# Seven half-sized products in place of eight for the gate and up products of four feed-forwards, with SBUF pools reopened by phase

## The chip, the cores and the metric

The kernel runs on one core of one Trainium2 chip. The metric is the device time of one execution in microseconds, median of three runs; lower is better. Before the change it is 1921.75 us (1920.16 to 1924.55).

## The reference, cut to what matters

A decoder trunk of two layers works on 512 tokens with 1024 features. Each layer has a feed-forward, a mixer and a second feed-forward, each added to the residual stream x (the feed-forwards with a factor of one half). The mixer of layer 0 is a gated linear recurrence, that of layer 1 a stick-breaking attention over keys and values that are projected once, from x after layer 0.

```python
D_MODEL, SEQ, D_FF = 1024, 512, 2816

def swiglu(h, w13, w2):
    gate, up = jnp.split(h @ w13, 2, axis=-1)
    return (jax.nn.silu(gate) * up) @ w2

for l in range(2):
    if l == 1:
        k_shared, v_shared = shared_kv(x, kv_norm, w_kv, k_norm)
    x = x + 0.5 * swiglu(rms_norm(x, ffn1_norm[l]), ffn1_w13[l], ffn1_w2[l])
    h = rms_norm(x, mix_norm[l])
    x = x + (rglru_block(h, ...) if l == 0 else stick_breaking_block(h, k_shared, v_shared, ...))
    x = x + 0.5 * swiglu(rms_norm(x, ffn2_norm[l]), ffn2_w13[l], ffn2_w2[l])
```

All data are float32.

## The kernel before, in words

Features lie on partitions and tokens along the free axis: x is eight tiles of 128 x 512. Each operand of a product is kept as two parts, a rounded one (hi, type fp32r) and the rest (lo). A product of weights and activations is three matmuls for each 128-wide step of the contraction: hi·hi, hi·lo, lo·hi (`steps`, lines 157 to 165). So a 128 x 512 output tile over 1024 features is 8 x 3 = 24 matmuls with 512 moving columns each, all recorded at line 111 (`mm`).

A feed-forward (`ffn`, lines 231 to 267) has 22 tiles of hidden features, cut into thirds of 8, 8 and 6. For each hidden tile it computes one gate tile and one up tile (two PSUM banks, 48 matmuls), then `swish`: VectorE multiplies both by the norm's factors r, ScalarE applies silu, VectorE multiplies the two, ScalarE rounds the product to hi and VectorE subtracts for lo. After a third's hidden tiles come eight down products, and VectorE adds each to x. With the last third, `after` squares the new x tile and splits x times gain into the next step's h. The factors r of the norm come after the first products (`Norm.rstd`), so the products run on x times gain without r.

Weights come in chunks of 128 x 1024 (`Weights`, lines 41 to 89): SyncE issues a DMA of 512 KB into a raw tile, ScalarE (or GpSimd) copies it to hi (line 55), VectorE subtracts for lo (line 59). Three buffers of each kind serve the whole program, and a chunk is emitted two chunks ahead of its use (`get`).

SBUF tiles come from pools that stay open for the whole program. In a pool, tiles of one tag share a number of buffers; a tile waits until a buffer of its tag is free, and buffers go out in the order in which they come free. The tiles h lie under tags `ah` and `al` (8 buffers each), the hidden tiles under `ch` and `cl` (8 each), temporaries `t0` and `t1` have two buffers each. PSUM has 8 banks under one tag.

The order of the instructions on each engine is made by the framework's list scheduler, which follows program order as priority among the instructions that its own estimate finds ready; two places fix it by hand (`manual_schedule`): the start and the first queries. On the chip each engine then keeps that order.

Between ffn2 of layer 0 and ffn1 of layer 1 stand the products of keys (8 x 24 matmuls) and values (192 matmuls). `v_out(1)` (lines 544 to 552), which evicts the second half of the values from PSUM, splits it and sends it to DRAM from two buffers of `t3` and two of `t4`, is called inside ffn1 of layer 1 after its first gate and up products, which need only h.

Of the kernel before, what the change touches and what calls it, by code (L numbers as in the profile page):

```python
# [12 lines left out]
P = 128  # L13
# [5 lines left out]
THIRDS = ((0, 8), (8, 16), (16, 22))  # L19
NH = 16  # L20
# [4 lines left out]
# queries of EARLY pairs come before the attention, the others among its units: from which step on, in how many steps  # L25
# [4 lines left out]
# columns of the packed vectors  # L30
# [4 lines left out]
# products of the recurrent block: inputs of the recurrence, its gates by block, the gate branch  # L35
# [5 lines left out]
class Weights:  # L41
    """Weight chunks in the order of their use: loaded ahead and split exactly into two 12-bit parts."""

    def __init__(self, nc, pool, plan, ahead):
        self.nc, self.pool, self.plan, self.ahead = nc, pool, plan, ahead
        self.ready, self.at = [], 0

    def tiles(self, j):
        return [self.pool.tile([P, 1024], dt, tag=t, name=f"{t}{j}") for t, dt in (("w_raw", F32), ("w_hi", F32R), ("w_lo", F32R))]
# [11 lines left out]
    def _emit(self, j):  # L61
        key, src, cols, hi_eng, lo_eng = self.plan[j]
        tiles = self.tiles(j)
        self.nc.sync.dma_start(tiles[0][:, :cols], src)
# [17 lines left out]
    def get(self, key):  # L82
        while len(self.ready) < min(len(self.plan), self.at + 1 + self.ahead):
# [5 lines left out]
        return hi, lo  # L89


@with_exitstack
def trunk(ctx, tc, a, out):
# [4 lines left out]
    hp = ctx.enter_context(tc.tile_pool(name="hp", bufs=8))  # L98
    wp = ctx.enter_context(tc.tile_pool(name="wp", bufs=3))
    tp = ctx.enter_context(tc.tile_pool(name="tp", bufs=2))  # L100
# [5 lines left out]

    def temp(tag, name, dt=F32, bufs=2, shape=None):
        return tp.tile(shape or [P, S], dt, tag=tag, name=name, bufs=bufs)
# [10 lines left out]
    plan = []  # L119
# [4 lines left out]
    def plan_ffn(n, l):  # L124
        for lo, hi in THIRDS:
            for i in range(lo, hi):
                plan_w((n, l, "g", i), a[f"{n}_w13"][l, i])
                plan_w((n, l, "u", i), a[f"{n}_w13"][l, FT + i])
# [3 lines left out]
    plan_ffn("ffn1", 0)  # L132
    for kind, m in RG_ORDER:
        plan_w((kind, m), a["w_ri"][m] if kind == "ri" else a["w_in"][m + (KT if kind == "rec" else 0)], hi="pool" if kind == "rec" else "act")
    for m in range(KT):
        plan_w(("wout", m), a["w_out"][m])
    plan_ffn("ffn2", 0)
# [5 lines left out]
    plan_ffn("ffn1", 1)  # L143
    for p in range(NPAIR):
        plan_w(("q", p), a["w_q"][p], hi="act" if p == 5 else "pool", lo="pool" if p == 5 else "dve")
    for m in range(KT):
        plan_w(("wo", m), a["w_o"][m], hi="pool" if m < 2 else "act")
    plan_ffn("ffn2", 1)
    W = Weights(nc, wp, plan, 2)

# [6 lines left out]
    def steps(ps, wt, ht, n=KT):  # L157
        """The products of ps = w.T h over n tiles of the contraction, w and h in two parts."""
# [12 lines left out]
    def product2(pa, wa, pb, wb, ht, full):  # L171
        """Two products of the same h; its last tile (or, in full, every tile) comes at the same time in both."""
# [6 lines left out]
    class Norm:  # L179
        """Sum of squares over the features of x and x * gain in two parts, tile by tile."""  # L180
# [15 lines left out]
        def rstd(self):  # L196
# [4 lines left out]
            # one table set for both functions, loaded between the last use of another and here  # L201
# [12 lines left out]
    def split_gain(xt, g, tag, name):  # L214
        hi = hp.tile([P, S], F32R, tag=tag + "h", name=name + "h")
        lo = hp.tile([P, S], F32R, tag=tag + "l", name=name + "l")
# [4 lines left out]
    def split(xt, tag, name, pool=False):  # L221
        hi = hp.tile([P, S], F32R, tag=tag + "h", name=name + "h")
        lo = hp.tile([P, S], F32R, tag=tag + "l", name=name + "l")
# [7 lines left out]
    def ffn(n, l, ht, rs, after, full=False):  # L231
        """x += 0.5 swiglu; rs() gives the norm's factors; after(m, x tile) once a tile of x is final."""
        r, queue = None, []

        def swish(i, pg, pu, act):
            tg, tu = temp("t0", f"tg{n}{l}{i}"), temp("t1", f"tu{n}{l}{i}")
# [4 lines left out]
            act.append(split(tu, "c", f"a{n}{l}{i}"))  # L241

        for lo_t, hi_t in THIRDS:
            act = []
            for i in range(lo_t, hi_t):
                pg, pu = psum(f"pg{n}{l}{i}"), psum(f"pu{n}{l}{i}")
# [30 lines left out]
    # the tensor engine's clock rises while the first data come in  # L277
# [15 lines left out]

    with tc.manual_schedule(engines={mybir.EngineType.DVE, mybir.EngineType.SP, mybir.EngineType.Activation}):
# [8 lines left out]
    def constants():  # L303
# [20 lines left out]
        # 0 where the key comes strictly before the query, else -1e30  # L324
# [28 lines left out]
        # gains of the per-head norms with the factors of the last Newton step (and 1/sqrt(head) for q)  # L353
# [6 lines left out]
    ffn("ffn1", 0, h, start, lambda m, t: n1.add(m, t, [(G_MIX[0], "a", h1)]), full=True)  # L360
# [6 lines left out]
    def conv(m, ps):  # L367
# [3 lines left out]
        xc[m] = hp.tile([P, S], F32, tag="bh", name=f"xc{m}")  # L371
# [20 lines left out]
    # p = tanh(-log_a / 2), q = 1 / (1 + p): a = 2 q - 1, sqrt(1 - a^2) = 2 sqrt(p) q  # L392
# [24 lines left out]
    def lru_3(b):  # L417
        for m in (2 * b, 2 * b + 1):
# [3 lines left out]
            hs[m] = hp.tile([P, S], F32, tag="bl", name=f"hs{m}")  # L422
# [43 lines left out]
    ffn("ffn2", 0, h2, n2.rstd, lambda m, t: n3.add(m, t, [(G_KV, "b", hkv), (G_FFN1[1], "a", h3)]))  # L466

# [6 lines left out]
    def head_norm(ps, r, g, name, dst, tags, qt=None):  # L474
        """psum * r, normed over each head's 64 rows, in two parts, to DRAM or to queries' tile qt; a generator of three stages."""
# [22 lines left out]
        if qt is not None:  # L498
            # both heads' rows in both halves of the partitions
# [20 lines left out]
    for p in range(NPAIR):  # L520
# [3 lines left out]
        if r3 is None:  # L524
            r3 = n3.rstd()
            # the same factors with tokens on partitions
# [12 lines left out]
        gen = head_norm(ps, r3, kg, f"k{p}", kd[p], ((tp, "t3"), (tp, "t4"), (tp, "rec"), (tp, "rec")))  # L539
# [34 lines left out]
    n4, h4 = Norm("n4"), []  # L574
    def finish_v():
        v_out(1, pvs[1])
        return r3
# [8 lines left out]
    ffn("ffn1", 1, h3, finish_v, after_ffn1)  # L586
# [8 lines left out]
    def load_pair(p):  # L595
        """Queries in both halves of the partitions; keys' two parts one above the other; values by chunk of keys."""
# [6 lines left out]
        for e in range(2):  # L603
            t = hp.tile([P, S], F32R, tag="cl", name=f"kp{p}{e}")
# [3 lines left out]
        for e in range(2):  # L608
            t = hp.tile([P, NCH, P], F32R, tag="cl", name=f"vp{p}{e}")
# [261 lines left out]
```

## Time and profile before

| | us |
|---|---|
| runs: median (lowest to highest) | 1921.75 (1920.16 to 1924.55) |
| profiled execution, span from first to last instruction | 1921.6 |
| TensorE matmuls busy | 1891.2 (98%), 8376 instructions |
| TensorE weight loads (beside the matmuls) | 1550.0 (81%), 8376 |
| VectorE busy | 1042.8 (54%), 1351 |
| ScalarE busy | 734.7 (38%), 1018 |
| GpSimd busy | 157.8 (8%), 196 |
| mean granted TensorE clock | 0.997 |

For the profiled execution no time is given apart from its span. Busy time of TensorE is taken from modelled ends, so two matmuls overlap in the records: the distance between the starts of neighbours is the time that one really takes. The same holds for VectorE, where the next instruction starts somewhat before the one before has ended in the records.

### The profile page before, as it was taken

To read this page: it belongs to the slowest core of one execution; us is meant where nothing else is said; L and a number is where in the kernel's file an instruction comes from. 1 tells how busy PE (TensorE), PEld (TensorE's weight loads), DVE (VectorE), ACT (ScalarE), POOL (GpSimd) and SP (SyncE) were. 2 spreads that over 40 slices of the span, in tenths; PEclk is the share of its full clock that TensorE was granted. 3 is DMA by queue.
4 is the path that set the end of the run, shared out by engine and by line. 5 is a ranking of instruction groups with operands and counts; after the bars stand their busy time and mean duration, and the time that the engine had idled before them with its cause. 6 is when DMAs were issued, how large, how long until landed. Compare 5 with 4: busy or idle time off the path is not lost.

```text
span 1921.6 us, 21311 instructions
## 1 busy us (share of the span) xinstructions
PE 1891.2 (98%) x8376; PEld 1550.0 (81%) x8376; DVE 1042.8 (54%) x1351; ACT 734.7 (38%) x1018; POOL 157.8 (8%) x196
## 2 busy tenths in 40 slices
PE   9999999999999999999999999999898999999999
PEld 7888888878788888888888888888676788888887
DVE  7434434797744354348744444346799854444343
ACT  6223223467543132236532223223588643222131
POOL 1000000031000000000200000000466400000000
PEclk9999999999999999999999999999999999999999
DMA  5322332322322233323562323324466222333322
GB/s 173 103 97 92 97 99 86 102 88 77 110 99 90 97 99 99 99 83 104 175 186 99 99 90 97 99 94 140 151 178 162 99 96 94 95 99 99 99 91 85
DMA packets 73092, 207.49 MB, mean 108 GB/s; under 512 B 7584, under 2 KB 17056, under 8 KB 72480
## 3 DMA queue, kind: packets, MB, share of 16 engines
q1 hardware_dynamic: 72704, 205.81, 33.8%
q8 instruction: 65, 1.06, 0.2%
q10 hardware_dynamic: 288, 0.32, 0.0%
q14 instruction: 35, 0.29, 0.0%
HBM read 189.85 MB, written 16.25 MB: 107 GB/s over the span
## 4 chain that ended last, share of the span: by engine, by line
PE 87%; DVE 7%; issue 2%; ACT 2%; POOL 2%; DMA 0%; POOLq 0%; DVEq 0%; ACTq 0%
PE pdffn L111 25%; PE pgffn L111 25%; PE puffn L111 25%; PE k L111 2%; PE v L111 2%; PE wout L111 2%; PE wo L111 2%; PE rec L111 2%; DVE spl L664 1%; DVE w_lo L59 1%; DVE t L664 1%; DVE sp L654 1%; PE z L111 1%; PE q L111 0%; POOL sph L661 0%
## 5 line engine op out<-in xcount | busy, mean ns | idle before, releaser
L55 ACT CAST w_hi<-w_raw 128x1024 fp32r<-128x1024 f32 (+1 forms) x313 | 321.4, 1030 | 979.4 <-PE pgffn L111 305.7
L59 DVE TENSOR_TENSOR w_lo<-w_raw,w_hi 128x1024 fp32r<-128x1024 f32 (+3 forms) x339 | 400.3, 1182 | 77.9 <-ACT w_hi L55 68.2
L239 DVE TENSOR_TENSOR tuffn<-puffn,rs_n 128x512 f32<-128x512 f32 x88 | 60.8, 691 | 242.3 <-PE puffn L111 242.3
L237 DVE TENSOR_TENSOR tgffn<-pgffn,rs_n 128x512 f32<-128x512 f32 x88 | 60.8, 691 | 216.1 <-PE pgffn L111 216.0
L265 DVE SCALAR_TENSOR_TENSOR x<-pdffn,x 128x512 f32<-128x512 f32 x72 | 49.8, 692 | 173.0 <-PE pdffn L111 172.8
L57 POOL TENSOR_SCALAR w_hi<-w_raw 128x1024 fp32r<-128x1024 f32 (+2 forms) x27 | 24.3, 903 | 751.5 <-PE pdffn L111 728.4
L240 DVE TENSOR_TENSOR tuffn<-tuffn,tgffn 128x512 f32<-128x512 f32 x88 | 60.7, 690 | 6.9
L238 ACT ACTIVATE tgffn<-tgffn 128x512 f32<-128x512 f32 x88 | 55.2, 627 | 5.4 <-DVE tgffn L237 5.1
L265 DVE SCALAR_TENSOR_TENSOR xr<-pdffn,xr 128x512 f32<-128x512 f32 x24 | 16.6, 692 | 70.9 <-PE pdffn L111 70.9
L481 POOL TENSOR_SCALAR thk<-tk 128x512 fp32r<-128x512 f32 x8 | 11.1, 1391 | 428.7 <-ACT tk L478 428.7
L111 PE MATMUL O<-t,vp 128*128 128x512 f32 (+1 forms) x144 | 41.2, 369 | 3.3 <-POOL t L661 1.9
L661 POOL TENSOR_SCALAR sph<-sp 128x512 fp32r<-128x512 f32 (+1 forms) x48 | 38.3, 802 | 23.4 <-DVE sp L657 12.8
L664 DVE TENSOR_TENSOR spl<-sp,sph 128x512 fp32r<-128x512 f32 (+1 forms) x48 | 38.8, 815 | 0.7 <-POOL sph L661 0.5
L661 POOL TENSOR_SCALAR t<-w 128x512 fp32r<-128x512 f32 (+1 forms) x48 | 37.5, 782 | 18.9 <-ACT w L685 15.7
L664 DVE TENSOR_TENSOR t<-w,t 128x512 fp32r<-128x512 f32 (+1 forms) x48 | 34.4, 717 | 3.3 <-POOL t L661 3.3
L111 PE MATMUL z<-qp,kp 128*128 128x256 f32 x192 | 33.5, 286 | 2.6 <-DVE qp L506 2.6
L111 PEld LDWEIGHTS z<-qp,kp 128*128 128x128 f32 x192 | 29.9, 191 | 6.3 <-DVE qp L506 3.4
L111 PEld LDWEIGHTS O<-t,vp 128*128 128x128 f32 x144 | 24.7, 188 | 11.1 <-DVE t L664 4.9
L187 ACT ACTIVATE sq_n<-x 128x512 f32<-128x512 f32 x40 | 25.1, 632 | 21.7 <-DVE x L265 18.0
L685 ACT ACTIVATE w<-z 128x512 f32<-128x512 f32 (+1 forms) x48 | 25.2, 525 | 16.2 <-PE z L111 15.5
L192 DVE TENSOR_TENSOR acc_n<-acc_n,sq_n 128x512 f32<-128x512 f32 x42 | 28.7, 684 | 0.1
L654 DVE SCALAR_TENSOR_TENSOR sp<-z,E 128x512 f32<-128x512 f32 (+1 forms) x48 | 28.3, 589 | 0.1
(1776 smaller groups left out, 5343.4 us busy)
## 6 DMA issues: line engine op xcount, KB each, us to landing
w_raw<-in_ffn_w SPq DMA_DIRECT2D x238, 512.0 KB, 3.3
w_raw<-in_ffn_w SPq DMA_DIRECT2D x32, 384.0 KB, 3.1
w_raw<-in_w_in SPq DMA_DIRECT2D x16, 512.0 KB, 3.2
qp<-qd SPq DMA_DIRECT2D x14, 512.0 KB, 5.4
w_raw<-in_w_out SPq DMA_DIRECT2D x8, 512.0 KB, 3.3
w_raw<-in_w_k SPq DMA_DIRECT2D x8, 512.0 KB, 3.2
w_raw<-in_w_v SPq DMA_DIRECT2D x8, 512.0 KB, 3.3
kp<-kd SPq DMA_DIRECT2D x32, 128.0 KB, 5.1
```

The costliest lines, as they stand in the source:

```text
L55: nc.scalar.copy(out=hi[:, cs], in_=raw[:, cs])
L59: eng.tensor_tensor(out=lo[:, cs], in0=raw[:, cs], in1=hi[:, cs].bitcast(F32), op=ALU.subtract)
L111: nc.tensor.matmul(o, l, r, start=start, stop=stop, skip_group_check=True)
L192: nc.vector.tensor_tensor(out=self.acc, in0=self.acc, in1=sq, op=ALU.add)
L237: nc.vector.tensor_tensor(out=tg, in0=pg, in1=r, op=ALU.mult)
L238: last_silu.append(nc.scalar.activation(out=tg, in_=tg, func=AF.Silu))
L239: nc.vector.tensor_tensor(out=tu, in0=pu, in1=r, op=ALU.mult)
L240: nc.vector.tensor_tensor(out=tu, in0=tu, in1=tg, op=ALU.mult)
L265: nc.vector.scalar_tensor_tensor(out=x[m], in0=pd, scalar=0.5, in1=x[m], op0=ALU.mult, op1=ALU.add)
L654: nc.vector.scalar_tensor_tensor(out=self.sp, in0=self.z, scalar=0.0, in1=ee, op0=ALU.max, op1=ALU.add)
L661: nc.gpsimd.tensor_scalar(out=hi, in0=src, scalar1=1.0, scalar2=0.0, op0=ALU.mult, op1=ALU.add)
L664: nc.vector.tensor_tensor(out=lo, in0=src, in1=hi.bitcast(F32), op=ALU.subtract)
```

## The change

The change works on pairs of hidden tiles. In 38 of the 44 pairs (11 in each of the four feed-forwards) the gate and up products of two tiles are computed by Strassen's scheme in the Winograd form: the weight matrix of the pair is cut into four blocks (two tiles of outputs by even and odd steps of the contraction), the activations into four blocks (even and odd steps by two halves of the tokens, 256 columns each), and seven products of blocks replace eight. The other six pairs (`PLAIN` = 4 tiles in three feed-forwards) stay as they were.

- The four blocks of a pair come by four DMAs of 512 KB, as before four chunks did. VectorE forms four sums of weight blocks (128 x 1024 each), and seven blocks in place of four are split into hi and lo. The pool has 7 raw, 5 hi and 5 lo buffers and works four chunks ahead in the feed-forwards, 3, 3, 3 and two in the mixers.
- A form (one of the seven products) is 2 (gate, up) x 4 steps x 3 = 24 matmuls of 256 columns. Seven forms use three PSUM banks; after each of the first six ScalarE or VectorE reads the bank into a tile `e`.
- Activations have to be normed and combined first: `normed` is called four times in a feed-forward (two tiles of x each) and makes seven blocks of 256 columns in two parts, with a tile `e` of 8 KB as scratch. It is called after the plain tiles (one call after each); in ffn1 of layer 1, which has no plain tiles, all four calls stand after `v_out(1)`, ahead of the first form. h for that feed-forward is no longer made.
- `swish`, `pair` and `normed` all take their scratch from one tag `e` with two buffers. Hidden tiles take the tags `ah` and `al`, the same eight buffers each as h.
- Pools for the activations' blocks, the weights and the scratch are opened and closed by phase; they lie on memory of the phase before, and a new tile waits for the tiles that lay there.

```diff
+PLAIN = {("ffn1", 0): 4, ("ffn2", 0): 4, ("ffn1", 1): 0, ("ffn2", 1): 4}
+BLOCKS = ("a11", "a21", "a22", "a12")
+SUMS = {"s3": ("a11", "a21"), "s1": ("a21", "a22"), "s2": ("s1", "a11"), "s4": ("s2", "a12"), **{b: None for b in BLOCKS}}
+FORMS = (("a11", "X", 4), ("s3", "Y", 0), ("s2", "X", 1), ("a12", "Z", 5), ("s1", "X", 2), ("a22", "Y", 3), ("s4", "X", 6))
+HS = S // 2
...
+    def block(self, j, name, src):
+        g = self.group
+        if name == FORMS[0][0]:
+            g.clear()
+            for k, b in enumerate(BLOCKS):
+                g[b] = self.tile("w_raw", f"w_{b}_{j}")
+                self.nc.sync.dma_start(g[b], src[k])
+        if name not in g:
+            p, q = SUMS[name]
+            p, q = (self.block(j, t, src) for t in (p, q))
+            g[name] = self.tile("w_raw", f"w_{name}_{j}")
+            self.nc.vector.tensor_tensor(out=g[name], in0=p, in1=q, op=ALU.add)
+        return g[name]
...
+    def phase_ffn():
+        close_pools()
+        cur.ht = open_pool("ht", hh=4, hl=4)
+        W.scope(open_pool("wf", w_raw=7, w_hi=5, w_lo=5), 4, plan_marks.pop(0))
+        cur.ep = None
+    def phase_mix():
+        close_pools()
+        cur.hp = open_pool("hp", bh=8, bl=8, ch=8, cl=8)
+        W.scope(open_pool("wm", w_raw=3, w_hi=3, w_lo=3), 2, plan_marks.pop(0))
+        cur.tp = open_pool("tp")
...
+    def normed(j, g, r, name):
+        e = cur.ep.tile([P, 8, HS], F32, tag="e", name=f"e{name}{j}")
+        for k in range(2):
+            xt = x[2 * j + k].rearrange("p (c t) -> p c t", c=2)
+            nc.vector.scalar_tensor_tensor(out=e[:, 2 * k:2 * k + 2], in0=xt, scalar=gain(g, 2 * j + k), in1=r.rearrange("p (c t) -> p c t", c=2), op0=ALU.mult, op1=ALU.mult)
+        hi = cur.ht.tile([P, 7, HS], F32R, tag="hh", name=f"hh{name}{j}")
+        lo = cur.ht.tile([P, 7, HS], F32R, tag="hl", name=f"hl{name}{j}")
...
+        nc.scalar.copy(out=hi[:, 4:6], in_=both)
+        nc.vector.tensor_tensor(out=lo[:, 4:6], in0=both, in1=hi[:, 4:6].bitcast(F32), op=ALU.subtract)
+        for o, p, q, op in ((t3, b22, b12, ALU.subtract), (t2, t3, b11, ALU.subtract), (t5, b11, b12, ALU.add), (t4, t2, b21, ALU.add)):
+            nc.vector.tensor_tensor(out=o, in0=p, in1=q, op=op)
+        nc.scalar.copy(out=hi[:, 0:4], in_=e[:, 4:8])
+        nc.vector.tensor_tensor(out=lo[:, 0:4], in0=e[:, 4:8], in1=hi[:, 0:4].bitcast(F32), op=ALU.subtract)
+        nc.scalar.mul(hi[:, 6], b22, -1.0)
+        nc.vector.scalar_tensor_tensor(out=lo[:, 6], in0=b22, scalar=-1.0, in1=hi[:, 6].bitcast(F32), op0=ALU.mult, op1=ALU.subtract)
...
         def swish(i, pg, pu, act):
-            tg, tu = temp("t0", f"tg{n}{l}{i}"), temp("t1", f"tu{n}{l}{i}")
+            e = cur.ep.tile([P, 4, S], F32, tag="e", name=f"e{n}{l}{i}")
+            tg, tu = e[:, 0], e[:, 1]
...
-            act.append(split(tu, "c", f"a{n}{l}{i}"))
+            act.append(split(tu, "a", f"a{n}{l}{i}"))
+        def pair(i, act):
+            banks = {}
+            e = cur.ep.tile([P, 4, S], F32, tag="e", name=f"e{n}{l}{i}")
+            for f, (name, bank, form) in enumerate(FORMS):
+                hi, lo = W.get((n, l, i, name))
...
+                for c in range(2):
+                    o = ps[:, c * HS:(c + 1) * HS]
+                    for j in range(KT // 2):
+                        ws = slice(c * S + j * P, c * S + j * P + P)
+                        xh, xl = hn[j][0][:, form], hn[j][1][:, form]
+                        mm(o, hi[:, ws], xh, new and c == 0 and j == 0, False)
+                        mm(o, hi[:, ws], xl, False, False)
+                        mm(o, lo[:, ws], xh, False, j == KT // 2 - 1)
+                if f == 0:
+                    nc.scalar.copy(out=e[:, 0], in_=ps)
...
+                elif f == 5:
+                    nc.vector.tensor_tensor(out=e[:, 1], in0=ps, in1=e[:, 1], op=ALU.subtract)
+            ps = banks["X"]
+            nc.scalar.activation(out=e[:, 0:3, 0:HS], in_=e[:, 0:3, 0:HS], func=AF.Silu)
+            last_silu.append(nc.scalar.activation(out=e[:, 3, 0:HS], in_=ps[:, 0:HS], func=AF.Silu, scale=-1.0))
+            nc.vector.tensor_tensor(out=e[:, 0:3, 0:HS], in0=e[:, 0:3, 0:HS], in1=e[:, 0:3, HS:S], op=ALU.mult)
...
+            for k, v in ((0, e[:, 0:4:3, 0:HS]), (1, e[:, 1:3, 0:HS])):
+                hi = ap.tile([P, S], F32R, tag="ah", name=f"ah{n}{l}{i + k}")
+                lo = ap.tile([P, S], F32R, tag="al", name=f"al{n}{l}{i + k}")
...
                 while queue:
                     swish(*queue.pop(0))
+                while len(hn) < (KT // 2 if i == nf - 1 else min(i + 1, KT // 2)):
+                    hn.append(normed(len(hn), g, r, f"{n}{l}"))
...
     n4, h4 = Norm("n4"), []
-    def finish_v():
-        v_out(1, pvs[1])
-        return r3
+    v_out(1, pvs[1])
+    close_pools(2)
+    cur.ep = open_pool("ep", e=2)
+    for j in range(KT // 2):
+        h3.append(normed(j, G_FFN1[1], r3, "n3"))
...
-    ffn("ffn1", 1, h3, finish_v, after_ffn1)
+    ffn("ffn1", 1, None, G_FFN1[1], None, after_ffn1, hn=h3)
+    phase_mix()
```

## Rows read from the trace of the kernel before

**Rows 1.** The page, part 1: busy us (share of the span) and instructions of each engine.
```profile
PE 1891.2 (98%) x8376; PEld 1550.0 (81%) x8376; DVE 1042.8 (54%) x1351; ACT 734.7 (38%) x1018; POOL 157.8 (8%) x196
```

**Rows 2.** The page, part 4: the chain that ended last, share by engine.
```profile
PE 87%; DVE 7%; issue 2%; ACT 2%; POOL 2%; DMA 0%; POOLq 0%; DVEq 0%; ACTq 0%
```

**Rows 3.** Windows: length, busy us by engine (PE, PEld, DVE, ACT, POOL), clock, DMA share, GB/s.
```profile
558.00:600.00 42.00, 42.00 (x187) 34.80 (x186) 19.32 (x25) 12.69 (x16) 0.00 (x0) 1.00 0.30 100
620.00:663.00 43.00, 43.00 (x192) 35.60 (x191) 16.54 (x18) 8.91 (x9) 0.00 (x0) 1.00 0.31 98
```

**Rows 4.** Timeline of TensorE, fourth hidden tile of ffn2, layer 0: start, duration, what.
```profile
570.88 0.39 PE L111 MATMUL puffn<-n2a0h,w_hi 128*128 128x512 f32 x1
...
576.32 0.39 PE L111 MATMUL pgffn<-n2a0h,w_hi 128*128 128x512 f32 x1
```

**Rows 5.** Timeline of TensorE in the attention: products of 256 columns.
```profile
1374.84 0.64 PE L111 MATMUL z<-qp,kp 128*128 128x256 f32 x4
1375.31 0.40 PE L111 MATMUL q<-n4a0h,w_hi 128*128 128x512 f32 x1
...
1393.33 0.65 PE L111 MATMUL z<-qp,kp 128*128 128x256 f32 x4
...
1394.53 0.40 PE L111 MATMUL O<-t,vp 128*128 128x512 f32 x1
```

**Rows 6.** Timeline of TensorE's weight loads in the attention.
```profile
1374.61 0.66 PEld L111 LDWEIGHTS z<-qp,kp 128*128 128x128 f32 x4
```

**Rows 7.** Lines by form, VectorE and ScalarE: operation, tiles, shapes, count, busy, mean ns.
```profile
L59 DVE TENSOR_TENSOR w_lo<-w_raw,w_hi 128x1024 fp32r<-128x1024 f32 x297 | 365.6, 1232 | 75.2 <-ACT w_hi L55 67.9 <-POOL w_hi L57 7.1
...
L59 DVE TENSOR_TENSOR w_lo<-w_raw,w_hi 128x768 fp32r<-128x768 f32 x32 | 30.6, 958 | 0.3 <-ACT w_hi L55 0.3
...
L654 DVE SCALAR_TENSOR_TENSOR sp<-z,E 128x256 f32<-128x256 f32 x16 | 6.6, 411 | 0.0
...
L55 ACT CAST w_hi<-w_raw 128x1024 fp32r<-128x1024 f32 x281 | 294.5, 1052 | 905.0 <-PE pgffn L111 296.3 <-PE pdffn L111 273.8 <-issue 203.1
L238 ACT ACTIVATE tgffn<-tgffn 128x512 f32<-128x512 f32 x88 | 55.2, 627 | 5.4 <-DVE tgffn L237 5.1
```

**Rows 8.** Timeline of VectorE: neighbours without a wait between them.
```profile
35.40 0.68 DVE L239 TENSOR_TENSOR tuffn<-puffn,rs_n 128x512 f32<-128x512 f32 x1
35.99 0.68 DVE L237 TENSOR_TENSOR tgffn<-pgffn,rs_n 128x512 f32<-128x512 f32 x1
...
567.04 1.22 DVE L59 TENSOR_TENSOR w_lo<-w_raw,w_hi 128x1024 fp32r<-128x1024 f32 x1
568.18 0.68 DVE L228 TENSOR_TENSOR affn202l<-tuffn,affn202h 128x512 fp32r<-128x512 f32 x1
```

**Rows 9.** Timeline of VectorE, ffn2 of layer 0: the factors r are complete.
```profile
550.16 0.43 DVE L211 TENSOR_SCALAR rs_n<-rs_n 128x512 f32<-128x512 f32 x1
```

**Rows 10.** Timeline of TensorE, ffn1 of layer 0: its fourth up product, and the next tile.
```profile
46.99 0.39 PE L111 MATMUL puffn<-h_0h,w_hi 128*128 128x512 f32 x1
...
52.43 0.39 PE L111 MATMUL pgffn<-h_0h,w_hi 128*128 128x512 f32 x1
```

**Rows 11.** Timeline of TensorE in the recurrent block: a wait.
```profile
427.46 0.97 PE L111 MATMUL ri<-xc4h,w_hi 128*128 128x512 f32 x3 [3.89 <-ACT xc4h L227]
```

**Rows 12.** Windows after this wait and after one at the attention's start.
```profile
430.00:440.00 10.00, 10.00 (x35) 7.92 (x34) 7.57 (x10) 3.51 (x4) 0.10 (x1) 0.73 0.16 55
...
1368.70:1380.00 11.30, 10.44 (x47) 8.88 (x48) 7.66 (x13) 8.01 (x16) 2.66 (x4) 0.85 0.29 93
```

**Rows 13.** Timelines at the end of the values: TensorE's next product.
```profile
985.55 0.39 PE L111 MATMUL pgffn<-n3a0h,w_hi 128*128 128x512 f32 x1
```

**Rows 14.** Timeline of VectorE there: the last split of the values.
```profile
989.66 0.75 DVE L550 SCALAR_TENSOR_TENSOR vl<-v,rc,vh 128x512 fp32r<-128x512 f32 x1 [0.90 <-DMA vd<-vl]
```

**Rows 15.** DMA issues: count, KB each, median us to landing.
```profile
w_raw<-in_ffn_w SPq DMA_DIRECT2D x238, 512.0 KB, 3.3
...
vd<-vl SPq DMA_DIRECT2D x8, 256.0 KB, 4.7
```

More of the change, by code (lines that the diff above doesn't have):

```diff
@@ L1 @@
-from contextlib import ExitStack
+from types import SimpleNamespace
 import concourse.bass as bass
@@ L41, with __init__, scope, tile @@
 class Weights:
-    def __init__(self, nc, pool, plan, ahead):
-        self.nc, self.pool, self.plan, self.ahead = nc, pool, plan, ahead
+    def __init__(self, nc, plan):
+        self.nc, self.plan = nc, plan
         self.ready, self.at = [], 0
+        self.pool, self.ahead, self.limit, self.group = None, 2, 0, {}
+    def scope(self, pool, ahead, limit):
+        assert self.at == len(self.ready) == self.limit
+        self.pool, self.ahead, self.limit = pool, ahead, limit
+    def tile(self, tag, name):
+        return self.pool.tile([P, 1024], F32 if tag == "w_raw" else F32R, tag=tag, name=name)
     def tiles(self, j):
-        return [self.pool.tile([P, 1024], dt, tag=t, name=f"{t}{j}") for t, dt in (("w_raw", F32), ("w_hi", F32R), ("w_lo", F32R))]
+        return [self.tile(t, f"{t}{j}") for t in ("w_raw", "w_hi", "w_lo")]
     def split(self, tiles, cs, hi_eng, lo_eng):
@@ L82, in get @@
     def get(self, key):
-        while len(self.ready) < min(len(self.plan), self.at + 1 + self.ahead):
+        while len(self.ready) < min(self.limit, self.at + 1 + self.ahead):
             self._emit(len(self.ready))
@@ L89, in get, with __init__, tile @@
         return hi, lo
+class Pool:
+    def __init__(self, pool, bufs):
+        self.pool, self.bufs = pool, bufs
+    def tile(self, shape, dt, tag, name, bufs=None):
+        return self.pool.tile(shape, dt, tag=tag, name=name, bufs=bufs or self.bufs.get(tag, 2))
 @with_exitstack
@@ L229, in split, with ffn @@
         return hi, lo
-    def ffn(n, l, ht, rs, after, full=False):
-        r, queue = None, []
+    def normed(j, g, r, name):
[5 more added lines that the diff above has]
+        lo = cur.ht.tile([P, 7, HS], F32R, tag="hl", name=f"hl{name}{j}")
+        b11, b12, b21, b22 = (e[:, k] for k in range(4))
+        t3, t2, t5, t4 = (e[:, 4 + k] for k in range(4))
+        both = e[:, 0:4].rearrange("p (k c) t -> p k c t", c=2)[:, :, 0]
+        nc.scalar.copy(out=hi[:, 4:6], in_=both)
[6 more added lines that the diff above has]
+        nc.vector.scalar_tensor_tensor(out=lo[:, 6], in0=b22, scalar=-1.0, in1=hi[:, 6].bitcast(F32), op0=ALU.mult, op1=ALU.subtract)
+        return hi, lo
+    def ffn(n, l, ht, g, rs, after, full=False, hn=None):
+        r, queue, nf = None, [], PLAIN[n, l]
+        hn = [] if hn is None else hn
         def swish(i, pg, pu, act):
-            tg, tu = temp("t0", f"tg{n}{l}{i}"), temp("t1", f"tu{n}{l}{i}")
+            e = cur.ep.tile([P, 4, S], F32, tag="e", name=f"e{n}{l}{i}")
+            tg, tu = e[:, 0], e[:, 1]
             nc.vector.tensor_tensor(out=tg, in0=pg, in1=r, op=ALU.mult)
@@ L359, in trunk @@
     n1, h1 = Norm("n1"), []
-    ffn("ffn1", 0, h, start, lambda m, t: n1.add(m, t, [(G_MIX[0], "a", h1)]), full=True)
+    ffn("ffn1", 0, h, G_FFN1[0], start, lambda m, t: n1.add(m, t, [(G_MIX[0], "a", h1)]), full=True)
     ntri, nrest, ident, nones, blk, mask, c4, cm8, kg, qg = (late[n] for n in ("ntri", "nrest", "ident", "nones", "blk", "mask", "c4", "cm8", "kg", "qg"))
+    phase_mix()
     r1 = None
@@ L603, in load_pair @@
         for e in range(2):
-            t = hp.tile([P, S], F32R, tag="cl", name=f"kp{p}{e}")
+            t = cur.hp.tile([P, S], F32R, tag="cl", name=f"kp{p}{e}")
             for j in range(2):
@@ L608, in load_pair @@
         for e in range(2):
-            t = hp.tile([P, NCH, P], F32R, tag="cl", name=f"vp{p}{e}")
+            t = cur.hp.tile([P, NCH, P], F32R, tag="cl", name=f"vp{p}{e}")
             nc.sync.dma_start(t.bitcast(F32), vd[p][e])
@@ L698, in values @@
                 if half == 1:
-                    pr.o = hp.tile([P, S], F32, tag="bh", name=f"o{pr.p}")
+                    pr.o = cur.hp.tile([P, S], F32, tag="bh", name=f"o{pr.p}")
                     os_.append(pr.o)
```

103 lines of the change are left out of this document (80 added, 23 removed).

## The prediction

> **What bounds the kernel now.** I read the busy shares first: TensorE's matmuls fill 98% of the span, and no other engine passes 54% [rows 1]. The chain of waits says the same: 87% of the span runs through TensorE [rows 2]. Modelled ends can hide gaps, so the timeline comes next: in a plain hidden tile the up product starts at 570.88 and the next product at 576.32, so 24 matmuls of 512 columns take 5.44 us, 226.7 ns each, without a gap [rows 4]. The windows show what the others have left: in 42 us of gate and up products VectorE works 19.3 us, ScalarE 12.7, DMA has a share of 0.30; in 43 us of down products VectorE works 16.5 [rows 3]. So here time goes only with TensorE's matmuls, until something else makes it wait.
>
> **The products.** A pair of hidden tiles costs 96 matmuls of 512 columns now: 96 x 226.7 ns = 21.76 us [rows 4]. After the change it costs 7 x 24 = 168 matmuls of 256 columns. The attention has such matmuls, with a weight load for each: four take 1375.31 - 1374.84 = 0.47 us (117.5 ns each), ten take 1394.53 - 1393.33 = 1.20 us (120 ns each) [rows 5]. I take 118.5: 168 x 118.5 ns = 19.91 us, 1.85 us less for a pair. For 38 pairs that is 70.5 us; at 117.5 it is 77, at 120 it is 61.
>
> Perfetto Trace Analysis, section "Identifying the Most-Contended Engine", in the Trainium skill speaks against this: it says to judge TensorE by the busy share of weight loads and not of matmuls. That share is 81% here [rows 1], and by mean record (185 ns) the 2736 added loads would bring it above the span. The rows on which it can be weighed are those of 256 columns, whose matmuls follow at 118 ns though the load of each has a record of its own; I follow them.
>
> **VectorE beside the pairs.** In the records an instruction's successor starts earlier than its end: 0.59 us after a 128x512 operation, 1.14 us after a 128x1024 one [rows 8]; with durations of 0.96 for 768 columns and 0.41 for 256 [rows 7] and the same overlap of 0.09, these cost 0.87 and 0.32. Per pair VectorE has 7 splits and 4 sums of 1024 columns (12.5 us), three bank reads (1.8), two products of 768 and 256 columns (1.2) and two splits (1.2): 16.7 us in 19.9 us of TensorE, 84%. ScalarE has seven copies of 1.05 us and some seven operations near 0.6 [rows 7], 11.7 us. Both stay under TensorE, so I cost them at nothing; the cover is thin on VectorE, and if it is late by 5% of its work in each pair, all 38 pairs lose up to 0.8 us each, 30 us. DMA brings the same four blocks of 512 KB in the same time; a load lands in 3.3 us [rows 15], and four chunks ahead are 11.4 us. SyncE's queue holds nothing else in these stretches. The down products do not change.
>
> **From plain tiles to pairs, three times.** Here I see the largest new wait. A pair's first form needs all four `normed` results. One costs VectorE 2 x 0.60 + 0.60 + 4 x 0.32 + 1.14 + 0.32 = 4.5 us [rows 7, 8]. Its scratch `e` has two buffers, shared with `swish`. `swish` of tile 0 keeps its buffer until it can write its hidden tile, and that lies under the tag of h, whose eight tiles are all in use until the fourth up product reads h0. In ffn2 of layer 0 the factors r are there at 550.6 [rows 9]; `swish` 0 and `normed` 0 take the two buffers, `swish` 1 takes the second one after it, and both then hold until h0 is free. That is three matmuls and their drain after 570.88, about 571.7 [rows 4]. From there, in program order on VectorE: two splits of the held tiles (after a ScalarE copy of 0.63 [rows 7], until 573.6), `normed` 1 (4.5), `swish` 2 (2.4), `normed` 2 (4.5), `swish` 3 (2.4), and of `normed` 3 the 2.6 us up to the two blocks that the first form reads: about 590. TensorE is free at 576.3 [rows 4] and waits 13.8 us, in which it can do the first steps of up to three forms (1.1 to 3.2 us): 12 us lost. The same holds for ffn2 of layer 1. In ffn1 of layer 0 r comes after two tiles, so `swish` 0 and 1 take both buffers and `normed` 0 waits too: h0 is free near 47.8, and 1.9 + 2 x 4.5 + 2.4 + 4.5 + 2.4 + 2.6 us later it is 70.7, against TensorE free at 52.4 [rows 10]: 18.3 less the same first steps, 16.5 us. Together 40.5 us. Low end: if the second buffer served `normed` all the while, only the last call would be late, some 3 us each, 9. High end: nothing done ahead and two weight splits (2.3 us) in between each time, 55.
>
> After a wait TensorE is slower for a while: after 3.89 us of idle [rows 11] the granted clock is 0.73 of full over the next 10 us, at the lower of its two levels for part of it, and after a shorter wait 0.85 over 11 us [rows 12], 2.7 and 1.7 us lost. I take 2 for each of the three: 6 us.
>
> **The start of ffn1 in layer 1.** Before, its first product follows the values at once (985.55 [rows 13]) and `v_out(1)` runs beside it. Now all four `normed` must come first; r and x have been there since the keys, and VectorE has room under the values, but the scratch lies on memory that `v_out(1)` uses. Its last split starts at 989.66 [rows 14], its transfer takes 4.7 us [rows 15], so that memory is free at 995.1. Of the two buffers one lies on the `t3` and `t4` of that call, the other on tiles used up by the keys. If the second one serves all four, nothing is lost. If one call needs the first, its blocks are there at 995.1 + 2.6 = 997.7: 12 us. If all four wait, 995.1 + 3 x 4.5 + 2.6 = 1011: 25 us. The rows do not say which; I take 6, between the two cheap ends.
>
> **Smaller edits.** After a pair's last form there are a silu (0.4), a product (0.4), a copy (0.6) and a split (0.7), 2.1 us with hops and perhaps a 1.1 us weight split ahead. The down products of the third cover it with the six earlier tiles of eight (18 x 0.227 = 4.1 us), but in a third of six only with four (2.7 us): about 1 us, four times. At the two entries into a mixer a first weight split (1.2 us) can wait for the last down product, as its memory is reused: 1 us each. Together 6 (bounds 0 and 25). The rest (hidden tiles under the tag of h at a third's end, values' h under the same tag) waits for single steps of a down product and is covered by the steps after it.
>
> **Sum.** 70.5 - 40.5 - 6 - 6 - 6 = 12 us gained. Against the span of 1921.6 this gives 1909.6; the median of the runs lies 0.15 above that span, so I say 1910 us. The likeliest case by itself spans 1896 to 1924.
>
> **Rivals.**
>
> The waits don't come: the scheduler finds an order in which `normed` runs under the plain tiles and under the values. For it: VectorE is idle for more than half of these stretches [rows 3]. Against it: two buffers, and h0's life. Then 9 us for the three starts, 0 for the clock and ffn1, 6 for the rest: 70.5 - 15 = 55.5, 1866 us.
>
> Slower, by VectorE: the starts cost 55 and 8 with the clock, ffn1 in layer 1 waits for all four calls (25), and a VectorE at 84% whose order was fixed by estimates makes each pair late. The point from which this decides: with starts at 40.5, clock 6 and small edits 6, 18 us are left; 25 us for ffn1 use them up, and every 0.1 us by which VectorE delays a pair adds 3.8 us. With 0.2 us a pair: 70.5 - 55 - 8 - 25 - 6 - 8 = -31.5, 1953 us; without the high end for the starts (40.5 and 6), 1937.
>
> The products don't shrink: a 256-column matmul in a long row is held by its weight load. In the rows four loads have records of 0.66 us together [rows 6], 165 ns each, though part of that is ahead of the first matmul. At 165 ns a pair costs 27.7 us, 6 more than before, and 38 pairs 226: some 2147 us before any wait. Against it: the distances of 118 in [rows 5].
>
> TensorE: Matmul & The Clock Gate, section "Back-to-back issue gap", in the Trainium skill goes the same way: it has 81 ns for a sustained pair of load and matmul at 128 columns and 131 at 512, which as an estimate makes 98 at 256, three quarters and not half. The trace has 226.7 and 118, about half, so it does not bear that out here.
>
> **How the numbers follow.** The forecast has 0.42, the waits that don't come 0.22, slower by VectorE 0.33, held by loads 0.03. A measurement of this kernel tells 0.2%, about 4 us, from no change. Of the forecast's 0.42, 0.31 lie faster, 0.08 within, 0.03 slower; of the third case 0.02 lie within. So faster 0.53, same 0.10, slower 0.37. The range reaches to the first rival and almost to the far end of the second: 1866 to 1950.
>
> **What would show it.** Starts of neighbouring matmuls in a pair 118 ns apart, a form 2.85 us: near 2.72 (half of 5.44) I was too careful, above 3.1 the gain is gone. Between the last plain up product and the first form, a wait of TensorE for the lines of `normed`, 10 to 18 us, three times, and a lower granted clock right after it. At the end of the values a wait of 0, 12 or 25 us. VectorE's busy share in stretches of pairs 80 to 90%, with few waits of TensorE on sums or splits. The prediction is wrong if the starts show no wait, or if TensorE waits inside the pairs.

## The result, and the profile after

The changed kernel takes 1982.73 us (median of four runs, 1978.94 to 1984.73), beside 1922.38 for the kernel before on the same chip. The ratio is 1.031, with a 95% interval of 1.0294 to 1.0324: slower by 3%. The forecast was 1910, and the range up to 1950 does not reach the result. The profiled execution has a span of 1983.0 us, against 1921.6 before.

The page of the kernel after comes first: busy times (it answers to [rows 1]), then its DMA queue, its HBM traffic and its two largest groups of DMA issues ([rows 15]).

```profile
PE 1874.7 (95%) x11112; PEld 1654.3 (83%) x11112; DVE 1430.1 (72%) x1753; ACT 927.7 (47%) x1288; POOL 153.1 (8%) x196
...
q1 hardware_dynamic: 116480, 365.22, 56.1%
...
HBM read 349.24 MB, written 16.25 MB: 184 GB/s over the span
...
w_a<-in_ffn_s SPq DMA_DIRECT2D x456, 512.0 KB, 4.8
w_raw<-in_ffn_w SPq DMA_DIRECT2D x86, 512.0 KB, 5.2
```

The reader is to see the 456. There are 38 pairs with four blocks each, so 152 loads were due; each pair loads its blocks three times. The code says why. `block` clears the group and issues four DMAs whenever it is asked for `a11`, and for `s3` and for `s2` it asks itself for `a11`. The chunks that land beside them take 5.2 us where they took 3.3 [rows 15]. As the group is cleared, the sum `s1` is lost as well and is formed twice. So a pair has twelve DMAs and five sums, where the section on the change has four of each.

The products themselves are as the change intends. Two forms that follow each other in ffn2 of layer 0, timeline of TensorE (start, duration):

```profile
699.83 0.28 PE L183 MATMUL pXffn<-hhffn,w_hi 128*128 128x256 f32 x1
...
702.71 0.28 PE L183 MATMUL pZffn<-hhffn,w_hi 128*128 128x256 f32 x1
```

24 matmuls in 2.88 us are 120 ns each (118.5 in the forecast), and 6132 of the 6384 distances in pairs lie within 2 ns of it. A pair costs 168 x 0.120 = 20.16 us in place of 21.76 [rows 4]; 38 pairs give 60.8 us.

Where TensorE now waits, in one view: what its matmuls waited for, in us and times, over the whole span.

```profile
PE pXffn L183 <- ACT hhn L324: 18.2, 3, 17.4
PE pXffn L183 <- ACT hhffn L324: 12.3, 6, 3.1
PE pYffn L183 <- ACT hhffn L328: 7.5, 7, 1.6
PE pgffn L183 <- ACT w_hi L73: 7.3, 2, 4.3
PE pYffn L183 <- DVE hlffn L329: 6.7, 6, 1.4
PE z L183 <- DVE spl L830: 6.6, 12, 1.6
PE q L183 <- DVE w_lo L77: 4.9, 1, 4.9
PE rec L183 <- DVE w_lo L77: 4.9, 1, 4.9
```

Lines 324 to 329 are `normed`: the first row is the start of ffn1 in layer 1, those of `hhffn` and `hlffn` are the three starts behind plain tiles. `q`, `rec` and `pg` are first products of a phase. Only the row of `z` has a counterpart of its size before (6.4 us there). Among the waits the clock is low. Windows of the kernel after (columns as in [rows 3]: length, busy times, and as the last three numbers the granted clock, the DMA share and GB/s): the first start in two parts, ffn2 of layer 0, the first pairs of ffn1 in layer 1, and 40 us of pairs only.

```profile
53.00:63.00 10.00, 5.49 (x18) 4.06 (x18) 10.00 (x21) 6.05 (x8) 0.00 (x0) 0.65 0.43 156
63.00:73.00 10.00, 3.46 (x10) 2.29 (x10) 10.00 (x21) 4.54 (x8) 0.00 (x0) 0.50 0.19 52
...
598.00:613.00 15.00, 6.48 (x20) 4.61 (x21) 15.00 (x28) 6.20 (x10) 0.00 (x0) 0.63 0.16 52
...
1028.90:1038.90 10.00, 6.49 (x24) 4.88 (x24) 10.00 (x20) 4.18 (x7) 0.00 (x0) 0.67 0.24 92
...
1060.00:1100.00 40.00, 40.00 (x335) 40.00 (x335) 30.80 (x34) 19.70 (x27) 0.00 (x0) 1.00 0.79 263
```

In the first four VectorE is busy from end to end and TensorE for 35 to 65% of the time, with the clock at 0.50 of full, the lower level, in the second one. In the last TensorE is full at full clock, though VectorE works 31 of 40 us and DMA has a share of 0.79.

The account below is worked out from the starts of all matmuls. For each kind of product it takes the distances between neighbours above their usual value (120 ns in pairs, 227 elsewhere) and puts each to the earlier of the two, so waits and slow clock stand together. Signs: plus is time lost against the kernel before.

| | forecast | kernel after |
|---|---|---|
| products of 38 pairs | -70.5 | -60.8 |
| three starts behind plain tiles, clock included | +46.5 | +47.3 (19.0, 14.4, 13.9) |
| start of ffn1 in layer 1 | +6 | +29.7 (17.6 to the first form, 12.1 in the first pairs) |
| other pairs (VectorE, DMA) | 0 | +9.8 |
| entries: `rec` 6.9, `q` 8.8, `wout` 3.2, `wo` 4.5, keys 4.3, first plain tiles 5.9, down products 1.2 | +6 | +34.8 |
| sum | -12 | +60.8 (the spans differ by 61.4) |

For the three starts the two can be told apart by size: distances above 0.3 us make 41.0 us, those up to 0.3 us, mostly 0.213, make 6.3. The forecast had 40.5 of waits and 6 for the clock. VectorE and ScalarE in ffn2 of layer 0 show why they wait. The factors r are complete at 570.1; here are the first call of `normed`, the end of the two held `swish`, and the second call:

```profile
571.33 1.40 DVE L318 SCALAR_TENSOR_TENSOR effn<-x,prm,rs_n 128x512 f32<-128x512 f32 x2
...
591.30 0.62 ACT L309 CAST affn200h<-effn 128x512 fp32r<-128x512 f32 x1
...
593.18 0.68 DVE L310 TENSOR_TENSOR affn201l<-effn,affn201h 128x512 fp32r<-128x512 f32 x1
593.78 1.41 DVE L318 SCALAR_TENSOR_TENSOR effn<-x,prm,rs_n 128x512 f32<-128x512 f32 x2
```

The fourth up product reads h0 for the last time at 590.83, and only then can `swish` 0 write its hidden tile. The second call of `normed` comes 22 us after the first, as the prediction had it, though VectorE stood idle for 2.5 us just before these splits.

### The profile page after: what moved, and what is told of

Its sections match the earlier page's. It is cut to its first block, busy times and chain, and to the rows that moved or that the text cites. A ratio compares the mean times of both kernels' runs of the same rounds, so it can differ in the third digit from the quotient of the medians.

```text
span 1983.0 us, 28034 instructions
## 1 busy us (share of the span) xinstructions
PE 1874.7 (95%) x11112; PEld 1654.3 (83%) x11112; DVE 1430.1 (72%) x1753; ACT 927.7 (47%) x1288; POOL 153.1 (8%) x196
## 5 line engine op out<-in xcount | busy, mean ns | idle before, releaser
L77 DVE TENSOR_TENSOR w_lo<-w_raw,w_hi 128x1024 fp32r<-128x1024 f32 (+3 forms) x187 | 213.4, 1148 | 70.3 <-ACT w_hi L73 53.2
L183 PE MATMUL pXffn<-hhffn,w_hi 128*128 128x256 f32 x864 | 249.0, 288 | 14.7 <-ACT hhffn L324 12.3
L183 PE MATMUL pXffn<-hlffn,w_hi 128*128 128x256 f32 x864 | 248.2, 287 | 1.5 <-DVE hlffn L325 0.9
L183 PE MATMUL pXffn<-hhffn,w_lo 128*128 128x256 f32 x864 | 246.7, 286 | 0.0
L183 PE MATMUL pdffn<-ahffn,w_hi 128*128 128x512 f32 x608 | 237.1, 390 | 0.3
L183 PE MATMUL pdffn<-alffn,w_hi 128*128 128x512 f32 x608 | 236.9, 390 | 0.0
L183 PE MATMUL pdffn<-ahffn,w_lo 128*128 128x512 f32 x608 | 236.6, 389 | 0.0
L77 DVE TENSOR_TENSOR w_lo<-w_s,w_hi 128x1024 fp32r<-128x1024 f32 x152 | 185.3, 1219 | 23.2 <-ACT w_hi L73 22.8
L183 PEld LDWEIGHTS pXffn<-hhffn,w_hi 128*128 128x128 f32 x864 | 168.1, 195 | 18.7 <-ACT hhffn L324 14.5
L183 PEld LDWEIGHTS pXffn<-hhffn,w_lo 128*128 128x128 f32 x864 | 168.2, 195 | 0.0
```

The costliest lines, as they stand in the source:

```text
L77: eng.tensor_tensor(out=lo[:, cs], in0=raw[:, cs], in1=hi[:, cs].bitcast(F32), op=ALU.subtract)
L183: nc.tensor.matmul(o, l, r, start=start, stop=stop, skip_group_check=True)
```

## Experiments

Theory T says that the time is lost at the seams and that TensorE hides the rest. Theory L says that the threefold loads and the fifth sum hold the pairs. The kernel before reads 1922.4 us beside the result and 1924.2 and 1923.4 us beside the two sets of experiments, so a gain taken across them is good to some 2 us.

**Blocks loaded once** (on the kernel after):

```diff
-        if name == FORMS[0][0]:
+        if name == FORMS[0][0] and src is not None:
...
-            p, q = (self.block(j, t, src) for t in (p, q))
+            p, q = (self.block(j, t, None) for t in (p, q))
```

> Each pair loads its four blocks once: 152 loads in place of 456, 152 sums in place of 190; nothing else is changed against the kernel after (1983 us). Theory T (the loss lies in waits at the seams: starts of the pairs, the end of the values, entries into phases; the threefold loads are hidden beside TensorE): between 1975 and 1985 us. The gaps at the three starts stay near 14, 11 and 11 us, since they wait for the lines of normed. Only the end of the values can gain, by some 4 us, because the stores of the values no longer stand behind block loads (a landing of 4.8 us goes back to about 3.3). Rival L (the loads and the extra sums hold the pairs: 69 us of TensorE starts above 120 ns lie within pairs): 20 to 40 us faster, 1943 to 1963 us, with the time coming out of the pairs.

Measured: 1963.63 us (1961.8 to 1964.38), ratio to before 1.0205 [1.019, 1.022]; 19.1 us faster than the kernel after. Its page has the loads and the traffic of the kernel before:

```profile
HBM read 189.85 MB, written 16.25 MB: 105 GB/s over the span
...
w_a<-in_ffn_s SPq DMA_DIRECT2D x152, 512.0 KB, 3.7
```

It lies between the two ranges: T's lower end missed by 11 us, L's upper end by 0.6. By the account most of the time came from two places, and some 6 us from the entries. The end of the values went from 17.6 to 10.5, for the waits there are now these (stretch at the end of the values; who waited for what, us, times, longest), first in the kernel after, then with blocks loaded once:

```profile
PE pXffn L183 <- ACT hhn L324: 17.4, 1, 17.4
...
ACT vh L712 <- DMA vd<-vh: 8.9, 2, 7.7
```

```profile
PE pXffn L183 <- ACT hhn L324: 10.2, 1, 10.2
...
DVE en L318 <- DMA vd<-vl: 3.2, 1, 3.2
```

ScalarE no longer waits 7.7 us for a store of the values to give a buffer back: in the kernel after eight block loads are issued in this stretch and a store lands in 5.1 us, with blocks loaded once it is one load and 3.5 us. The other place is the pairs, 69.2 to 59.9. The three starts kept their 19, 14 and 14, as T had it; what went is a wait here and there in later pairs. One of them in the kernel after (858 to 867 us):

```profile
ACT w_hi L73 <- DMA w_a<-in_ffn_s: 2.4, 1, 2.4
DVE w_s L101 <- DMA w_a<-in_ffn_s: 2.2, 1, 2.2
PEld pXffn L183 <- ACT effn L369: 0.9, 1, 0.9
```

ScalarE stands before a weight block that has not landed; the copy that empties a bank is queued behind it, and TensorE waits for that bank.

**Loads alone:** the blocks still come three times, but the sum `s1` is kept.

```diff
         if name == FORMS[0][0]:
-            g.clear()
+            if self.plan[j][0][-1] == name:
+                g.clear()
```

> The kernel after (1983 us) with its 456 block loads, but the sum s1 is kept, so that a pair has four sums and not five: 152 sums of weights in place of 190. This parts the 19 us that loading once gave. If the loads cost them (DMA traffic, buffers, the stores behind them): 1978 to 1984 us. If VectorE's fifth sum costs them (38 x 1.14 = 43 us of VectorE): 1962 to 1968 us.

Measured: 1981.89 us (1976.14 to 1984.8), ratio 1.0302 [1.0284, 1.032]. So the loads cost the 19 us, and the fifth sum, 38 x 1.14 = 43 us of VectorE, costs nothing that shows. Whether the loads cost by traffic or by the seven raw buffers through which they pass was not parted.

**`normed` ahead of `swish`** (on the kernel after, loads threefold):

```diff
+                while len(hn) < KT // 2:
+                    hn.append(normed(len(hn), g, r, f"{n}{l}"))
                 while queue:
                     swish(*queue.pop(0))
-                while len(hn) < (KT // 2 if i == nf - 1 else min(i + 1, KT // 2)):
-                    hn.append(normed(len(hn), g, r, f"{n}{l}"))
```

> All four calls of normed stand ahead of the first swish after r is known, so that they take the two scratch tiles e before a swish holds them; loads stay threefold. Theory T: the four calls are some 18 to 20 us of VectorE. In the two ffn2 they begin at r (about 550) and end near 569, before TensorE has finished its plain tiles (576): both gaps of 11 us and their spells at half clock go, 15 us each at most. In ffn1 of layer 0 r comes later and half of its 14 us stays. Together 25 to 35 us faster than 1983: 1948 to 1958. Rival L (starts wait for block loads and weight sums as well): gaps at the starts stay above 6 us each, gain under 12 us: above 1971. A second rival: the swish calls that are put off hold PSUM banks, and the plain tiles or the first form wait for a bank instead: no gain, 1978 to 1988.

Measured: 1966.41 us (1966.33 to 1969.82), ratio 1.0227 [1.021, 1.0244], 16.3 us faster than the kernel after. The three starts fell from 19.0, 14.4 and 13.9 to 15.0, 8.8 and 7.2, together 16.3. The direction is T's, the size is between T and L. In ffn1 of layer 0 the second rival shows in small: the first form waits 2.1 us for a bank that a put-off `swish` still has to read. In ffn2 of layer 0 (584 to 606 us) TensorE no longer waits for `normed` but for weights:

```profile
PE pXffn L183 <- ACT w_hi L73: 5.0, 1, 5.0
ACT w_hi L73 <- DVE w_s L101: 4.1, 2, 2.2
```

**Blocks for ffn1 of layer 1 made under the values** (on the kernel after):

```diff
-            hi, lo = temp("t3", f"vh{g}{s}", F32R), temp("t4", f"vl{g}{s}", F32R)
+            hi, lo = temp("sq", f"vh{g}{s}", F32R), temp("acc", f"vl{g}{s}", F32R)
...
+            if g == 0 and c == 1:
+                close_pools(2)
+                cur.ep = open_pool("ep", e=2)
+            if g == 0 and c >= 2 or g == 1 and c in (1, 2):
+                h3.append(normed(len(h3), G_FFN1[1], r3, "n3"))
...
     v_out(1, pvs[1])
-    close_pools(2)
-    cur.ep = open_pool("ep", e=2)
-    for j in range(KT // 2):
-        h3.append(normed(j, G_FFN1[1], r3, "n3"))
```

> The blocks of the activations for ffn1 of layer 1 are made while the values are computed: the values are evicted through the scratch of the norms (sq, acc), the scratch of the keys is closed after the last key, and the four calls of normed stand under the values. Theory T: the wait of 17.4 us at the end of the values goes, so do the six gaps behind it (8.4 us) and the stretch at half clock (about 10 us): 26 to 36 us faster than 1983, 1947 to 1957. Rival D (VectorE is the thing that is late: 18 us of normed now stand ahead of the splits of the values' weights): TensorE waits under the values instead, 5 to 15 us, and the gain is 10 to 20 us: 1963 to 1973.

Measured: 1956.87 us (1955.61 to 1958.33), ratio 1.0172 [1.0156, 1.0187]: 25.9 us faster, the lower edge of T. The values themselves lose nothing (44.42 us from the first to the last start of their 192 matmuls, 44.41 in the kernel after), so D falls. Windows of the values' last 48 us and of the first pairs:

```profile
962.00:1010.00 48.00, 47.77 (x210) 38.99 (x209) 43.58 (x64) 24.83 (x36) 3.52 (x5) 1.00 0.62 197
...
1012.00:1066.00 54.00, 48.98 (x400) 47.96 (x399) 43.61 (x46) 29.31 (x38) 0.00 (x0) 1.00 0.86 288
```

VectorE is busy for 43.6 of 48 us and TensorE still runs through. The first pairs then lose 5 us, at a DMA share of 0.86.

**The three edits together:**

> The three edits together: blocks loaded once, normed ahead of the first swish, blocks for ffn1 of layer 1 made under the values. Theory T: the gains add, 4 + 30 + 31 us off 1983: about 1918, between 1905 and 1930, what is left being the entries into the five phases (gaps of 5.2, 3.4, 3.0, 5.3 and 4.7 us) and ordinary pairs. Rival L: the pairs themselves gain as well, 1880 to 1900.

Measured: 1910.92 us (1909.72 to 1913.89), ratio 0.9935 [0.992, 0.995]: faster than before by 0.65%, in T's range. That this is also the 1910 of the forecast is chance, since it took three edits to get there. The gain is 71.8 us where the three alone add up to 61.3; of the waits for weights that the second and third edit ran into, most are gone with the extra loads. The first pairs of ffn1 in layer 1 lose 2.9 us now, and the starts 12.5, 1.7 and 0.0.

**Memory of the phases laid out anew** (on the three edits). Weights of a mixer lie on the dead blocks of the activations, weights of a feed-forward on dead scratch of the mixer; `Two` takes the pool by the tag's first letter, and the keys take their scratch from `e` (not shown):

```diff
     def phase_ffn():
         cur.ht = open_pool("ht", hh=4, hl=4)
+        cur.ep = open_pool("ep", e=2)
         W.scope(open_pool("wf", w_raw=7, w_hi=5, w_lo=5), 4, plan_marks.pop(0))
...
     def phase_mix():
-        cur.hp = open_pool("hp", bh=8, bl=8, ch=8, cl=8)
-        W.scope(open_pool("wm", w_raw=3, w_hi=3, w_lo=3), 2, plan_marks.pop(0))
+        wm = open_pool("wm", w_raw=3, w_hi=3, w_lo=3)
+        cur.hp = Two(open_pool("hc", ch=8, cl=8), open_pool("hb", bh=8, bl=8))
+        W.scope(wm, 2, plan_marks.pop(0))
```

> On top of the three edits together (1911 us) the memory of the phases is laid out anew: the weights of a mixer lie on the activations' blocks of the feed-forward before, which are dead since its last pair, and the weights of a feed-forward lie on scratch of the mixer that is dead before its output product; the scratch of the keys is taken from e. Theory T2 (at the entries the first weights wait for memory that the last products of the phase before still use): the gaps at the entries into the mixers (5.25 us twice) and into the two ffn2 (3.4 and 4.7 us) go below 1 us each, as in the kernel before, and with them the slow clock behind them: 16 to 26 us faster, 1885 to 1895 us. Rival Q (the first splits wait in VectorE's order behind the splits of h, whose buffers the hidden tiles of the last third hold under the same tags; memory has nothing to do with it): the gaps into the mixers stay above 3 us, gain under 10 us: 1901 to 1911.

Measured: 1885.8 us (1884.07 to 1887.47), ratio 0.9806 [0.9793, 0.9819]: 25.1 us faster than the three edits, as T2 had it. By the account `rec` went from 8.1 to 0.5, `q` from 12.1 to 6.2 (6.0 before the change), `wo` from 6.0 to 1.7, `wout` from 4.8 to 1.7, the first plain tiles from 8.0 to 4.0; the keys lose 1.1 more. What the trace of the three edits shows at first sight is Q's picture. VectorE at the entry into the recurrent block, kernel with the three edits (start, duration):

```profile
367.31 0.74 DVE L300 SCALAR_TENSOR_TENSOR n1a6l<-x,prm,n1a6h 128x512 fp32r<-128x512 f32 x1
...
370.02 0.75 DVE L300 SCALAR_TENSOR_TENSOR n1a7l<-x,prm,n1a7h 128x512 fp32r<-128x512 f32 x1
370.69 3.48 DVE L77 TENSOR_TENSOR w_lo<-w_raw,w_hi 128x1024 fp32r<-128x1024 f32 x3
```

The first weight split stands behind the last six splits of h, and TensorE's first product stops for it: its third matmul (371.96) starts 5.24 us after its second. But that order follows from the memory, since only the layout differs: with the new one the same split stands 17.7 us ahead of these splits of h, which come as late as ever (the first of them 2.44 us before TensorE's first product in both kernels), and TensorE starts that product at 365.31 and goes through it without a gap:

```profile
345.16 1.21 DVE L77 TENSOR_TENSOR w_lo<-w_raw,w_hi 128x1024 fp32r<-128x1024 f32 x1
...
362.87 0.75 DVE L309 SCALAR_TENSOR_TENSOR n1a2l<-x,prm,n1a2h 128x512 fp32r<-128x512 f32 x1 [0.75 <-ACT n1a2h L308]
```

**Six plain tiles in ffn1 of layer 0** (on the new layout):

```diff
-PLAIN = {("ffn1", 0): 4, ("ffn2", 0): 4, ("ffn1", 1): 0, ("ffn2", 1): 4}
+PLAIN = {("ffn1", 0): 6, ("ffn2", 0): 4, ("ffn1", 1): 0, ("ffn2", 1): 4}
```

> The new layout, and in ffn1 of layer 0 six plain tiles in place of four, so 37 pairs in place of 38. There the factors r come only after two plain tiles, and with four plain tiles the first pair still waits (gaps of 3.6 and 5.2 us, then a slow clock). A pair turned back into plain tiles costs 1.6 us; normed is covered by 10.9 us more of TensorE. Theory T: the two gaps go, 5 to 12 us faster than the new layout alone. Rival B: swish of tiles 2 to 5 cannot write hidden tiles before h is free, holds both tiles e and with them all PSUM banks, so that the first pair waits for a bank just the same: no gain, or 2 us slower.

Measured: 1880.15 us (1879.91 to 1881.3), ratio 0.9778 [0.9765, 0.9791], 5.65 us faster than the layout alone. That start fell from 10.0 to 1.4 us, one pair less costs 1.6, and rival B falls. With the new layout alone it had waited no longer for `normed`, but for a weight split on VectorE and for a bank (50 to 70 us):

```profile
PE pZffn L192 <- DVE w_lo L77: 5.0, 1, 5.0
...
PE pXffn L192 <- DVE effn L351: 2.5, 1, 2.5
```

The version with six plain tiles is the best: 43 us below the kernel before on the same chip (1923.42). Its busy times, and what its matmuls wait for most:

```profile
PE 1840.4 (98%) x11040; PEld 1633.6 (87%) x11040; DVE 1388.3 (74%) x1709; ACT 923.1 (49%) x1282; POOL 156.9 (8%) x196
```

```profile
PE z L192 <- DVE spl L836: 5.4, 11, 1.0
PE hsk L192 <- POOL ek L652: 4.0, 3, 2.6
PE ri L192 <- ACT xc4h L318: 3.9, 1, 3.9
```

Two of the three rows are waits of the mixers that the kernel before has as well (6.4 and 3.9 us there); the second belongs to the keys. No wait for `normed` or for a phase's first weights is among the first seven.

## Why the prediction was wrong

**The step that failed first** is "DMA brings the same four blocks of 512 KB in the same time". It was read from the list of loads in the plan and not from the calls: the recursion in `block` loads them three times. Cost: 19.1 us, shown by loading once and by the run with loads alone. It fell on the end of the values, on single pairs and on the entries, and it also kept the other edits from their full effect. The next two steps overlap with it, so each has its figure with blocks loaded once beside it. The prediction's own sign of being wrong, waits inside the pairs, came from here: 9.8 us in pairs behind the first ones, and nothing of it was left with blocks loaded once.

**"Smaller edits", 6 with bounds of 0 and 25:** 34.8 measured, the largest error, and 28.5 with blocks loaded once. The step gave each entry into a mixer 1 us for one weight split. The memory argument was right, but what is late is not one split: at the entry into the recurrent block it stands behind six splits of h on VectorE, the first of which themselves wait for down products to free hidden tiles. That the list scheduler chose this order by its estimate is not shown beyond the order itself. Nor did the step cost the entries into the feed-forwards and the keys. The run with the new layout gave 25.1 of it back.

**"The start of ffn1 in layer 1", 6 with ends of 0, 12 and 25:** 29.7. The high case was the true one: all four calls came behind the stores of `v_out(1)`. VectorE in the kernel after, from the last split of the values to the first call:

```profile
1020.10 1.46 DVE L713 SCALAR_TENSOR_TENSOR vl<-v,rc,vh 128x512 fp32r<-128x512 f32 x2
1024.43 2.48 DVE L101 TENSOR_TENSOR w_s<-w_a,w_a 128x1024 f32<-128x1024 f32 x2 [2.88 <-DMA vd<-vl]
1026.84 1.41 DVE L318 SCALAR_TENSOR_TENSOR en<-x,prm,rs_n 128x512 f32<-128x512 f32 x2
```

The first form waited 17.4 for the first call; the other calls held the first pairs, form by form and in part at a lower clock (12.1). With blocks loaded once it is 10.5 and 13.2, together 23.7, so the 25 was well priced and what it lacks to 29.7 is the loads. Choosing a value between the two cheap ends had no row behind it. Making the blocks under the values gave 25.9 back.

**"From plain tiles to pairs, three times", 40.5 and 6 for the clock:** 47.3, right in place, size and cause; only the shape differs, as the wait is not one before the first form but many in the steps of the first pair. That two scratch buffers held by `swish` are the cause is read from the trace (the second call of `normed` at 593.78) and borne out by the run with `normed` first: the three starts lost 16.3 us by an order alone, and nearly all in the two ffn2 once loads came once.

**The products, 70.5:** 60.8. The distance is 120 ns and not 118.5; the low bound of 61 was the value. No rival by weight loads: in the pairs a load has a record of 195 ns, as this row of the kernel after shows (count, busy, mean ns), and 168 of them would be 32.8 us, but a pair takes 20.16.

```profile
L183 PEld LDWEIGHTS pXffn<-hhffn,w_hi 128*128 128x128 f32 x864 | 168.1, 195 | 18.7 <-ACT hhffn L324 14.5
```

The Trainium skill, Perfetto Trace Analysis, section "Identifying the Most-Contended Engine", judges TensorE's headroom by the arithmetic done as a share of the peak and by the busy share of weight loads. In the window from 1060 to 1100 they fill 40.00 of 40 us, so by that share nothing is left there; the trace agrees as far as matmuls fill it too, but the records of loads overlap, and their sum does not give the time.

**VectorE at nothing** was right in the rows of pairs. In 40 us of pairs it is busy for 30.8 us, in a like window of the best version for 33.6; 43 us more of it (the fifth sum) did not show. It was not right for the first pair behind a seam, where weight splits and `normed` share VectorE: with the new layout one weight split still held it for 5.0 us. So the rival that ends slower had the sign and the high end of ffn1, but its deciding mechanism, pairs delayed by VectorE, did not occur. The rival without waits (1866) is nearly what the best version reaches by hand: 1880, with 120 ns in place of 118.5.

## What to carry to other kernels

A saving on the bound engine is paid at every seam where that engine's next input is made by others, so price each seam by its own queue: what stands ahead of the first input in program order, and which memory it waits for. Follow a helper's calls through to the DMAs that it issues and count them against the plan, since a repeated load leaves the result unchanged and shows in the page only as traffic and in the count of issues. Pools reopened by phase should lie on what died longest ago: here the order in which the pools are opened, with the keys' scratch moved to suit, gave 25 us.

## What the runs showed of the hardware

In rows of pairs 256-column matmuls with a weight load each follow at 120 ns, where 512 columns take 226.7; half would be 113.4. Whether the load makes the 6.6 ns was not tried. Waits cost more than their length: over 63 to 73 us, among waits of up to 3.4 us, the granted clock was 0.50, the lower of its two levels, and in the first pairs of the three starts slow matmuls made 6.3 us beside 41.0 of waits. Block loads of three times the bytes (456 in place of 152), at a DMA share of 0.79 and 263 GB/s, left 40 us of pairs at full speed, so their cost cannot be read from steady stretches.
